# Seven products for a second set of K tiles in wout2, a new set in the second layer's glu1 and glu2, and down rows turned sooner

## The chip, the cores and the metric

One core of a Trainium2 chip runs the whole program in one launch. The metric is the device time of one execution in microseconds. An instruction runs on TensorE (PE, matrix products; PEld is its weight load), VectorE (DVE), ScalarE (ACT), GpSimd (POOL) or SyncE (SP); here POOL and SP mostly start DMAs. Each engine works through its own list in order and waits for others by semaphores. A matmul takes a stationary 128x128 block and a moving block of up to 512 columns and adds into a PSUM bank.

## The reference

Two layers, float32, 256 tokens, width 2048. With `h = rmsnorm(x)`:

```python
proj = h @ w_in          # conv a, glu, gate; q and kv down-projection (512 + 512 + 64); 3 more gates
y_conv = conv_branch(c_a, c_glu, c_gate, ...) @ w_proj_conv   # 31 taps over time, layernorm, silu, gate
y_mla = mla_branch(rmsnorm(q_down) @ w_uq, rmsnorm(kv_down) @ w_ukv, ...) @ w_proj_mla  # 16 heads
y = sigmoid(g_conv) * y_conv + sigmoid(g_mla) * y_mla
return x + y @ w_out     # the next layer's x
```

Nearly all the work is products of 256 token rows with weights that are each read once.

## The kernel before

**Blocks, ticks, units.** A layer is a list of blocks of 512 output columns (`order_of_layer`): glu0, down0 to down2 (512, 320 and 256 columns), glu1, glu2, the attention's uq and ukv with glu3 to glu7 between them, the gates, gmla, gconv, pmla, pconv and last wout0 to wout3. A block's weights come in eight pieces of two K tiles (`KS = 2`), 128x1024 float32, 512 KB, one DMA on SP each. A piece that is multiplied is a unit: ACT copies it into a rounded `hi`, DVE subtracts to get `lo`, and TensorE makes three products for each of the two token tiles and two K tiles, hi x hi, hi x (low half of the activations) and lo x hi: 12 matmuls of 128x512, one tick. `background` stands ahead of each tick. It runs what `at_slot` has put down for that tick (evacuations, transposes, stores and fetches, with tick distances written as numbers), and fills what is left of the tick with convolution work from a queue by estimated costs; `assist` lets ACT multiply taps of the convolution that DVE then only adds, while ACT's own estimate leaves more than a threshold. `InOrder` keeps this order on each engine, so an instruction that waits holds up all behind it on its engine.

**Seven products.** Two neighbouring blocks ("left" and "right"), two token tiles and two pieces make a 2x2 product of 2x2 block matrices. It is done with seven products instead of eight (42 matmuls, not 48). `q1, q7, q6, q5` begin the sums and need weights added to one another (DVE: `sum<-raw,raw`, `sum<-sum,raw`, `raw<-raw,raw`) and sums of the activations (`make_forms`: `whole`, `differences`, `forms`). They stand in the four ticks `TAIL` of the block ahead, the host. `q2, q4, q3` finish the four sums in ticks 0, 2, 4 (`front`) of the block itself; DVE joins the partial sums (`joins`, `right`). The banks alternate between two homes. `SEVEN` lists the left blocks: gconv0, gconv2, pconv2, wout0, wout2 in both layers. The pieces that are left are plain ticks, 12 for a pair of blocks. So wout0 (with wout1) hosts the beginning of wout2 (with wout3).

**Turning rows.** A result has tokens on partitions, and the next product needs columns there. `turn` stores a 128x512 tile to DRAM in four DMAs of 64 KB (`park`), fetches it back rearranged (`fetch`, 256 KB, POOL) `fetch_at` ticks later, and `at` ticks after the store DVE transposes it in 32x32 blocks (STREAM_TRANSPOSE). One tick behind that, halves are split off: for the next layer's input ACT writes `hT0` and DVE `hT1` (SCALAR_TENSOR_TENSOR, 128x128, four per token tile). The output blocks use it through `turn4` with c = 0 to 3 for the block and t for the token tile; block c's rows are K tiles 4c to 4c+3 of the next layer's glu0. The down rows are scaled by DVE (`scaled(0)` for q, `scaled(1)` for kv) and turned through `turn` in place; uq and ukv need them.

Of the kernel before, what the change touches and what calls it, by code (L numbers as in the profile page):

```python
# [19 lines left out]
P = 128  # L20
# [52 lines left out]
SEVEN = {(l, kind, i) for l in range(DEPTH) for kind, i in (("gconv", 0), ("gconv", 2), ("pconv", 2), ("wout", 0), ("wout", 2))}  # L73
# [47 lines left out]
def trunk(ctx: ExitStack, tc: tile.TileContext, xT, x, g_in, pos, win, wuq, wukv, wpc, wpm, wo, cst, rows, invf, out):  # L121
# [68 lines left out]
    TAIL = {n: (-7, -5, -4, -3) for n in (8, 12, 16)}  # L190

    def plan_all():
        blocks = [(l, k, i, pieces_of(l, s)) for l in range(DEPTH) for k, i, s in order_of_layer()]
        seven, home = None, 0
        for at, (l, k, i, block) in enumerate(blocks):
            first = (l, k, i) in SEVEN
            woven = WOVEN.get((l, k, i))
# [10 lines left out]
            block.twin = bool(first or woven)  # L208
            js = woven or js
            after = at + 1 + block.twin  # L210
            following = blocks[after] if after < len(blocks) else None
            tail = []
            if following and following[:3] in SEVEN:
                tail = ["q1", "q7", "q6", "q5"]
                upcoming = SimpleNamespace(units={}, home=1 - home, banks={}, forms=None)
                upcoming.n = following[3].n
                upcoming.left, upcoming.right = following[3].pieces[:2], blocks[after + 1][3].pieces[:2]
            tails = dict(zip([len(js) + a for a in TAIL[len(js)]], tail)) if tail else {}
            block.begins = upcoming if tail else None
            for slot, (j, right) in enumerate(js):  # L220
                tick = []
                for q, of in ((front.get(slot), seven), (tails.get(slot), upcoming if tail else None)):
                    if q:
                        (b11, b21), (b12, b22) = of.left, of.right
                        raw, unit = (lambda a: ("raw", a)), (lambda a: ("unit", of.units[a]))
                        if q in ("q1", "q2", "q3"):
                            if q == "q3":
                                sources.append(sources[b22])
                                b22 = len(sources) - 1
                            of.units[q] = plain({"q1": b11, "q2": b21, "q3": b22}[q])  # L230
                        elif q == "q7":
                            of.units[q] = summed(of.n, (raw(b12), raw(b22)), None, [b12, b22])
                        elif q == "q6":
                            of.units[q] = summed(of.n, (unit("q7"), raw(b11)), unit("q7"), [])
                        elif q == "q5":
                            of.units[q] = summed(of.n, (raw(b12), raw(b11)), raw(b12), [])
                        else:
                            of.units[q] = summed(of.n, (unit("q6"), raw(b21)), unit("q6"), [])
                        tick.append((q, of.units[q], of))
# [122 lines left out]
    def background(n, extra=0):  # L362
# [24 lines left out]
        while assist and budget["act"] > 0.8 and assist[0]():  # L387
            budget["act"] -= 0.85
# [86 lines left out]
    def one_of_seven(q, i, of):  # L475
# [3 lines left out]
        if q in ("q1", "q2", "q4"):  # L479
            parts = [of.stat({"q1": 0, "q2": KS, "q4": KS}[q] + kk, int(q == "q4")) for kk in range(KS)]  # L480
        else:
            parts = [of.forms(q, kk) for kk in range(KS)]
        hi, lo, _ = done[i]
        begins = q in ("q1", "q7", "q6", "q5")
        terms = [(kk, p) for p in range(3) for kk in range(KS)]
        for m, (kk, part) in enumerate(terms):
# [4 lines left out]
            )  # L491
        if q == "q1":
# [317 lines left out]
    for l in range(DEPTH):  # L810
# [31 lines left out]
        def down_after(down=down, qkc=qkc, ss_d=ss_d, r_d=r_d, kpe=kpe, ccq=ccq, ssq_t=ssq_t, gqk=gqk, row=row, C=C, ss_base=ss_base):  # L842
# [14 lines left out]
            def scaled(i):  # L857
                for t in range(T):
# [4 lines left out]
                    turn(d, LORA, None, then=lambda z, t=t: separated(i, t, z), then_costs=(0.65, 0.65), at=7 + t, home=d, fetch_at=3)  # L863
# [26 lines left out]
            at_slot(5, factors, 2.6)  # L890
# [840 lines left out]
```

## Time and profile before

| | us |
|---|---|
| median of 3 runs (lowest to highest) | 1865.14 (1865.07 to 1865.27) |
| profiled execution: time / span of its instructions | 1864.87 / 1863.1 |
| PE busy | 1857.7 (100%), 8395 matmuls |
| DVE busy | 1711.9 (92%), 2662 instructions |
| ACT busy | 1358.3 (73%) |
| POOL busy | 494.4 (27%) |
| granted TensorE clock | 1.0 |

Matmuls are pipelined: the durations of their rows overlap, so PE's pace is read from how many start in a stretch. DVE and ACT rows also overlap a little (a row's duration holds some 0.08 us that the next row shares). "Idle before <- releaser" in a timeline is the time an engine stood ahead of that row, and what let it go on. All rows of the program carry one line number (L132 before), since one helper issues every instruction, so rows are told apart by the tiles they write and read. An x8 behind a row stands for eight like rows in sequence.

### The profile page before, as it was taken

The numbers are of one execution on the slowest core, as the hardware profiler recorded it, in microseconds if no ns is written. First come the engines' busy times: TensorE is split into PE (matmuls) and PEld (weight loads), VectorE is DVE, ScalarE is ACT, GpSimd is POOL, SyncE is SP. The second block draws the span as 40 slices with busy tenths as digits, with TensorE's granted clock in tenths as the row PEclk, the third lists the DMA queues.
The fourth block names the chain that finished last, engine by engine and source line by source line (L and its number), as shares of the span: only waits on it lengthen the run. The fifth ranks groups of instructions, "written<-read, shape, count | busy, mean of one in ns | idle before, by whom it ended". The sixth has DMA issues, their size and how long they took to land.

```text
span 1863.1 us, 26923 instructions
## 1 busy us (share of the span) xinstructions
PE 1857.7 (100%) x8395; PEld 1544.7 (83%) x8395; DVE 1711.9 (92%) x2662; ACT 1358.3 (73%) x2421; POOL 494.4 (27%) x942
## 2 busy tenths in 40 slices
PE   9999999999999999999999999999999999999999
PEld 8888888888888888888888888888888888888887
DVE  6999999899999999999769999989999999988995
ACT  7678888988886765555657688888888777665553
POOL 0154555542200000021421545655322000000211
PEclk9999999999999999999999999999999999999999
DMA  8777877877755666678977777887877566765785
GB/s 333 234 267 246 275 253 253 266 268 232 238 200 199 206 220 218 204 244 277 333 233 232 258 263 260 257 257 257 273 237 235 189 198 209 235 216 184 252 279 178
DMA packets 140400, 450.28 MB, mean 242 GB/s; under 512 B 23840, under 2 KB 29216, under 8 KB 140256
## 3 DMA queue, kind: packets, MB, share of 16 engines
q1 hardware_dynamic: 106416, 364.74, 59.2%
q0 software_dynamic: 32832, 82.62, 13.5%
q8 instruction: 66, 1.08, 0.2%
q10 hardware_dynamic: 1008, 1.20, 0.2%
q14 instruction: 78, 0.64, 0.1%
HBM read 404.43 MB, written 44.04 MB: 241 GB/s over the span
## 4 chain that ended last, share of the span: by engine, by line
PE 98%; DVE 2%; issue 0%; DVEq 0%
PE acc L132 73%; PE left L132 12%; PE right L132 11%; PE o_ps L132 1%; PE s1w L132 1%; DVE lo L132 1%; PE s L132 1%; DVE v_t L132 1%; PE warm L132 0%; PE acc_end L132 0%; DVE whole_a L132 0%; DVE sum L132 0%; DVE whole_b L132 0%; DVE form_b L132 0%; DVE forms L132 0%
## 5 line engine op out<-in xcount | busy, mean ns | idle before, releaser
L132 ACT CAST hi<-raw 128x1024 fp32r<-128x1024 f32 (+2 forms) x683 | 695.3, 1028 | 302.0 <-PE acc L132 168.0
L132 DVE TENSOR_TENSOR lo<-raw,hi 128x1024 fp32r<-128x1024 f32 (+2 forms) x667 | 798.9, 1204 | 95.4 <-ACT hi L132 32.3
L132 PE MATMUL acc<-hi,hT 128*128 128x512 f32 (+1 forms) x1472 | 357.7, 383 | 0.0
L132 PEld LDWEIGHTS acc<-hi,hT 128*128 128x128 f32 x1472 | 271.5, 188 | 53.5
L132 PE MATMUL acc<-hi,h_hi 128*128 128x512 f32 (+1 forms) x736 | 224.8, 386 | 0.0
L132 PE MATMUL acc<-hi,h_lo 128*128 128x512 f32 (+2 forms) x736 | 220.6, 381 | 0.0
L132 DVE SCALAR_TENSOR_TENSOR v_t<-u_t,cst,v_t 128x256 f32<-128x256 f32 x500 | 213.8, 479 | 2.9
L132 ACT ACTIVATE tap<-u_t,cst 128x256 f32<-128x256 f32 x460 | 200.7, 499 | 7.4 <-DVE v_t L132 7.4
L132 POOL DMA_DIRECT2D turned<-turn_d x88 | 49.2, 559 | 558.8 <-DVE v_t L132 362.2
L132 PE MATMUL acc<-lo,h_hi 128*128 128x512 f32 (+1 forms) x704 | 189.9, 386 | 0.0
L132 PE MATMUL acc<-lo,hT 128*128 128x512 f32 (+1 forms) x704 | 189.3, 386 | 0.3 <-DVE lo L132 0.3
L132 POOL DMA_DIRECT2D turn_d<-gate x184 | 100.2, 551 | 285.6 <-DVE gate L132 177.1
L132 DVE TENSOR_TENSOR v_t<-v_t,tap 128x512 f32<-128x512 f32 x230 | 157.8, 686 | 6.5
L132 PEld LDWEIGHTS acc<-hi,h_lo 128*128 128x128 f32 x736 | 137.4, 188 | 28.1 <-DVE h_lo L132 0.2
L132 PEld LDWEIGHTS acc<-hi,h_hi 128*128 128x128 f32 x736 | 135.9, 188 | 26.1 <-ACT h_hi L132 0.3
L132 PEld LDWEIGHTS acc<-lo,hT 128*128 128x128 f32 x704 | 131.1, 188 | 26.9 <-DVE lo L132 0.7
L132 PEld LDWEIGHTS acc<-lo,h_hi 128*128 128x128 f32 x704 | 130.9, 188 | 26.7 <-DVE lo L132 0.8
L132 PE MATMUL acc<-hi,oT 128*128 128x512 f32 x512 | 127.8, 389 | 0.0
L132 PE MATMUL acc<-hi,qkc 128*128 128x512 f32 x448 | 115.4, 389 | 0.0
L132 PEld LDWEIGHTS acc<-hi,oT 128*128 128x128 f32 x512 | 95.8, 188 | 19.7
L132 PEld LDWEIGHTS acc<-hi,qkc 128*128 128x128 f32 x448 | 83.5, 188 | 17.0
L132 POOL DMA_DIRECT2D turn_d<-su x128 | 70.0, 553 | 104.3 <-DVE su L132 89.1
(259 smaller groups left out, 2877.2 us busy)
## 6 DMA issues: line engine op xcount, KB each, us to landing
raw<-in_win SPq DMA_DIRECT2D x401, 512.0 KB, 4.3
raw<-in_wo SPq DMA_DIRECT2D x68, 512.0 KB, 5.5
raw<-in_wpc SPq DMA_DIRECT2D x66, 512.0 KB, 4.3
raw<-in_wpm SPq DMA_DIRECT2D x64, 512.0 KB, 3.6
raw<-in_wukv SPq DMA_DIRECT2D x32, 512.0 KB, 4.4
turned<-turn_d POOLq DMA_DIRECT2D x56, 256.0 KB, 4.7
raw<-in_wuq SPq DMA_DIRECT2D x24, 512.0 KB, 4.3
turn_d<-qk POOLq DMA_DIRECT2D x128, 96.0 KB, 4.5
```

Source lines behind the costliest of these rows:

```text
L132: ins = getattr(self.engine, name)(*a, **k)
```

## The change

Two groups of seven in wout2 (16 of 32 piece products of its pair, in place of 8) in both layers, with the two groups' sums joined only once; one group in the second layer's glu1 and glu2, begun in down0 of that layer and held in its banks over down1 and down2; the second group's forms in tiles of the pool `uv`; residual rows of c >= 2 in that pool too; c=1 of the output blocks turned at 5 ticks instead of 8; the second layer's down rows scaled one tick sooner, fetched 2 instead of 3 ticks after the store and turned 4 instead of 7; the assist threshold 0.4 instead of 0.8.

```diff
-SEVEN = {(l, kind, i) for l in range(DEPTH) for kind, i in (("gconv", 0), ("gconv", 2), ("pconv", 2), ("wout", 0), ("wout", 2))}
+SEVEN = {(l, kind, i): n for l in range(DEPTH) for kind, i, n in (("gconv", 0, 1), ("gconv", 2, 1), ("pconv", 2, 1), ("wout", 0, 1), ("wout", 2, 2))}
+SEVEN[1, "glu", 1] = 1
+BEGUN_IN = {("glu", 1): ("down", 0)}
...
-    TAIL = {n: (-7, -5, -4, -3) for n in (8, 12, 16)}
+    COMMON, OTHERS = ("q1", "q7", "q6", "q5"), ("q2", "q4", "q3")
+    TAIL = {1: ((-7, -5, -4, -3),), 2: ((-10, -9, -8, -7), (-6, -5, -4, -3))}
+    FRONT = {1: ((0, 2, 4),), 2: ((0, 2, 4), (1, 3, 5))}
...
-                js = js[2:] + [(j, True) for j, _ in js[2:]]
+                js = js[2 * quads :] + [(j, True) for j, _ in js[2 * quads :]]
...
-        while assist and budget["act"] > 0.8 and assist[0]():
+        while assist and budget["act"] > 0.4 and assist[0]():
...
+        begins = q in COMMON and quad is of.quads[0]
...
+        if quad is not of.quads[-1]:
+            return
         if q == "q1":
...
+                parts = [uv_p.tile([P, KS, SEQ], F32R, tag="uv", name=f"form{p}") for p in range(4)]
...
+            soon = int((l, "glu", 1) in SEVEN)
...
-                    turn(d, LORA, None, then=lambda z, t=t: separated(i, t, z), then_costs=(0.65, 0.65), at=7 + t, home=d, fetch_at=3)
+                    turn(d, LORA, None, then=lambda z, t=t: separated(i, t, z), then_costs=(0.65, 0.65), at=(4 if soon else 7) + t, home=d, fetch_at=3 - soon)
...
-            at_slot(5, factors, 2.6)
+            at_slot(5 - soon, factors, 2.6)
             for i in range(2):
-                at_slot(6 + 2 * i, lambda i=i: scaled(i), 1.3)
+                at_slot(6 - soon + (2 - soon) * i, lambda i=i: scaled(i), 1.3)
...
-                soon_at = {} if c == 1 else dict(fetch_at=3, at=6)
-                return turn(src, 512, None, then=use, then_costs=costs, **soon_at)
+                return turn(src, 512, None, then=use, then_costs=costs, fetch_at=at[c] // 2, at=at[c])
...
+                pool, tag = (uv_p, "uv") if c >= 2 else (wide_p, "w")
+                keep["x", c, t] = pool.tile([P, 512], F32, tag=tag, name="xres")
...
-            turn4(xt, c, t, use, 1.15, 1.3)
+            turn4(xt, c, t, use, 1.15, 1.3, at=(6, 5, 6))
...
-                product(pl, uses_h, lambda t, ps, i=i: glu_evac(i, t, ps), at, (0.9, 2.2), tardy=6 if i == 0 and l else None)
+                product(pl, uses_h, evac_of(glu_evac, i, pl), at, (0.9, 2.2), tardy=6 if i == 0 and l else None)
...
-                    at_slot(8, lambda i=i, f=wout_begin: f(i + 1))
+                    at_slot(len(pl.ticks) - 4, lambda i=i, f=wout_begin: f(i + 1))
```

Over the program TensorE gets 18 matmuls of 128x512 fewer (8377 for 8395), VectorE 15 instructions more (2677 for 2662), and SP three loads of 512 KB more.

Three places show how the order moves. DVE in the first layer's wout0, before (a row names what is written and what is read; the number behind a unit's `lo` counts units, and `raw` numbers are pieces):

```order
L132 TENSOR_TENSOR lo325_8708<-raw318_8604,hi325_8682 128x1024
L132 TENSOR_TENSOR gate_8726<-right_8088,sc_6647 128x512
L132 TENSOR_TENSOR gate_8726<-gate_8726,ym_5812 128x512
L132 STREAM_TRANSPOSE turned_8642<-turned_8642 128x512
L132 TENSOR_TENSOR yT1_8139<-turned_8619,yT0_8138 128x4x128
L132 TENSOR_TENSOR lo326_8737<-raw319_8628,hi326_8710 128x1024
L132 TENSOR_TENSOR lo327_8749<-raw683_8652,hi327_8739 128x1024
L132 TENSOR_TENSOR yT1_8139<-turned_8642,yT0_8138 128x4x128
L132 TENSOR_TENSOR lo328_8773<-raw312_8672,hi328_8751 128x1024
```

and the same place of the changed kernel:

```order
L134 TENSOR_TENSOR lo325_8744<-raw324_8638,hi325_8718 128x1024
L134 TENSOR_TENSOR sum327_8748<-raw332_8686,raw333_8688 128x1024
L134 TENSOR_TENSOR gate_8762<-right_8122,sc_6687 128x512
L134 TENSOR_TENSOR gate_8762<-gate_8762,ym_5838 128x512
L134 STREAM_TRANSPOSE turned_8676<-turned_8676 128x512
L134 TENSOR_TENSOR yT1_8173<-turned_8653,yT0_8172 128x4x128
L134 TENSOR_TENSOR lo326_8773<-raw318_8662,hi326_8746 128x1024
L134 TENSOR_TENSOR lo327_8785<-sum327_8748,hi327_8775 128x1024
L134 TENSOR_TENSOR lo328_8798<-raw319_8708,hi328_8787 128x1024
L134 TENSOR_TENSOR sum327_8748<-sum327_8748,raw324_8638 128x1024
L134 TENSOR_TENSOR whole_a_8817<-yT0_8172,yT1_8173 128x512
L134 TENSOR_TENSOR whole_b_8819<-yT0_8172,yT1_8173 128x512
```

The first common product (unit 325) now stands in the stage's first ticks, and its sums of weights and the second group's `whole` rows come between the low halves. Before, the first sum of weights came three rows below the last row shown.

DVE in the second layer's glu0, before (turned_9328 and 9330 are the rows of output block c=2, turned_9453 and 9455 of c=3; hT1 is the low half of the layer's input, which TensorE reads):

```order
L132 SCALAR_TENSOR_TENSOR hT1_8999<-turned_9328,gains_111,hT0_8998 128x128 x4
L132 SCALAR_TENSOR_TENSOR hT1_8999<-turned_9330,gains_111,hT0_8998 128x128 x4
L132 TENSOR_TENSOR lo359_9473<-raw344_9313,hi359_9437 128x1024
L132 TENSOR_TENSOR lo360_9491<-raw345_9344,hi360_9475 128x1024
L132 STREAM_TRANSPOSE turned_9453<-turned_9453 128x512
L132 STREAM_TRANSPOSE turned_9455<-turned_9455 128x512
L132 TENSOR_TENSOR lo361_9511<-raw346_9370,hi361_9493 128x1024
```

and in the changed kernel (c=2 in turned_9448 and 9450, c=3 in turned_9513 and 9515):

```order
L134 STREAM_TRANSPOSE turned_9448<-turned_9448 128x512
L134 STREAM_TRANSPOSE turned_9450<-turned_9450 128x512
L134 TENSOR_TENSOR lo363_9537<-raw345_9385,hi363_9519 128x1024
L134 STREAM_TRANSPOSE turned_9513<-turned_9513 128x512
L134 STREAM_TRANSPOSE turned_9515<-turned_9515 128x512
L134 SCALAR_TENSOR_TENSOR hT1_9098<-turned_9448,gains_111,hT0_9097 128x128 x4
L134 SCALAR_TENSOR_TENSOR hT1_9098<-turned_9450,gains_111,hT0_9097 128x128 x4
L134 TENSOR_TENSOR lo364_9573<-raw346_9420,hi364_9539 128x1024
```

The rows of c=2 that write hT1 stood four rows ahead of c=3's first transpose and now stand behind its second. On POOL the two fetches of c=2 move in the same way; before:

```order
L132 DMA turned_9328<-turn_d_9244 128x512
L132 DMA turn_d_9386<-xres_9286 32x4x128 x4
L132 DMA x1_dram_106<-xres_9286 128x512
L132 DMA x1_dram_106<-xres_9288 128x512
L132 DMA turned_9453<-turn_d_9386 128x512
```

and in the changed kernel:

```order
L134 DMA turn_d_9436<-xres_9286 32x4x128 x4
L134 DMA turned_9448<-turn_d_9324 128x512
L134 DMA turned_9450<-turn_d_9331 128x512
L134 DMA x1_dram_106<-xres_9286 128x512
L134 DMA x1_dram_106<-xres_9288 128x512
L134 DMA turned_9513<-turn_d_9436 128x512
```

The fetch of c=2 stood ahead of the store of c=3's rows and now stands behind it.

DVE where the second layer's down rows are turned, before (down1 holds the rows; two transposes for q, then two for kv; qkc1 is their low half):

```order
L132 TENSOR_TENSOR lo401_10444<-raw386_10302,hi401_10426 128x1024
L132 STREAM_TRANSPOSE down1_9403<-down1_9403 128x512
L132 TENSOR_TENSOR lo402_10467<-raw387_10334,hi402_10446 128x1024
L132 STREAM_TRANSPOSE down1_9403<-down1_9403 128x512
L132 TENSOR_TENSOR qkc1_9404<-down1_9403,qkc1_9404 128x4x128
L132 TENSOR_TENSOR lo403_10488<-raw388_10377,hi403_10469 128x1024
L132 STREAM_TRANSPOSE down1_9403<-down1_9403 128x512
```

and in the changed kernel:

```order
L134 TENSOR_TENSOR lo407_10522<-raw386_10387,hi407_10499 128x1024
L134 TENSOR_TENSOR kpe_9469<-ka_10237,kb_10238 128x2x32
L134 TENSOR_TENSOR kpe_9469<-kb_10238,ka_10237 128x2x32
L134 SCALAR_TENSOR_TENSOR ccq_9470<-cos2_109,down1_9465 128x128
L134 SCALAR_TENSOR_TENSOR ssq_t_9471<-sin2_110,down1_9465 128x128
L134 SCALAR_TENSOR_TENSOR gqk_9472<-cst_9464 128x1
L134 STREAM_TRANSPOSE down1_9465<-down1_9465 128x512
L134 TENSOR_TENSOR lo408_10549<-raw387_10399,hi408_10524 128x1024
L134 STREAM_TRANSPOSE down1_9465<-down1_9465 128x512 x2
L134 TENSOR_TENSOR qkc1_9466<-down1_9465,qkc1_9466 128x4x128
L134 TENSOR_TENSOR lo409_10571<-raw388_10429,hi409_10551 128x1024
```

The first transpose now comes four ticks behind the scaling of q, where it came seven behind, and the first of kv shares a tick with the second of q.

More of the change, by code (lines that the diff above doesn't have):

```diff
@@ L206, in plan_all @@
                 if k == "wout" and i == 0:
                     js.sort(key=lambda e: e[0] // 2)
[L208 to L239, printed above, removed]
@@ new lines, in plan_all @@
+            block.plain, block.twin, block.seven, block.begins = woven or js, bool(quads or woven), None, None
+            block.extra = [[] for _ in block.plain]
+            block.begun_in = block
+        home = 0
+        for at, (l, k, i, block) in enumerate(blocks):
+            if skipped(at) or (l, k, i) not in SEVEN:
+                continue
+            host = at - 1
+            while skipped(host) or (k, i) in BEGUN_IN and blocks[host][1:3] != BEGUN_IN[k, i]:
+                host -= 1
+            host = blocks[host][3]
+            home = 1 - (host.seven.home if host.seven else 0)
+            of = block.seven = host.begins = SimpleNamespace(kind=k, home=home, banks={}, first=None, last=None)
+            number = SEVEN[l, k, i]
+            of.quads = [
+                SimpleNamespace(
+                    of=of, c=c, n=block.n, units={}, left=block.pieces[2 * c : 2 * c + 2],
+                    right=blocks[at + 1][3].pieces[2 * c : 2 * c + 2],
+                )
+                for c in range(number)
+            ]
+            for quad, tail, front in zip(of.quads, TAIL[number], FRONT[number]):
+                for q, a in zip(COMMON, tail):
+                    host.extra[len(host.plain) + a].append((q, quad))
+                for q, a in zip(OTHERS, front):
+                    block.extra[a].insert(0, (q, quad))
@@ L240, in plan_all @@
+        for at, (l, k, i, block) in enumerate(blocks):
+            if skipped(at):
+                continue
+            for (j, right), extra in zip(block.plain, block.extra):
+                tick = [unit_of_seven(q, quad) for q, quad in extra]
                 tick.append((right, plain((blocks[at + 1][3] if right else block).pieces[j]), j))
                 block.ticks.append(tick)
-            if tail:
-                seven = upcoming
         return blocks
@@ L479, in one_of_seven @@
         if q in ("q1", "q2", "q4"):
-            parts = [of.stat({"q1": 0, "q2": KS, "q4": KS}[q] + kk, int(q == "q4")) for kk in range(KS)]
+            parts = [of.stat(2 * KS * quad.c + (KS if q != "q1" else 0) + kk, int(q == "q4")) for kk in range(KS)]
         else:
-            parts = [of.forms(q, kk) for kk in range(KS)]
+            parts = [quad.forms(q, kk) for kk in range(KS)]
         hi, lo, _ = done[i]
-        begins = q in ("q1", "q7", "q6", "q5")
+        begins = q in COMMON and quad is of.quads[0]
         terms = [(kk, p) for p in range(3) for kk in range(KS)]
@@ L840, in down_evac, with down_after @@
                 act.activation(dst, ps, AF.Copy, scale=r)
[L842 removed]
+        def down_after(l=l, down=down, qkc=qkc, ss_d=ss_d, r_d=r_d, kpe=kpe, ccq=ccq, ssq_t=ssq_t, gqk=gqk, row=row, C=C, ss_base=ss_base):
             ka = work.tile([P, T, ROPE], F32, tag="qa", name="ka")
@@ L1531, in trunk, with forms_of, forms_at @@
         h_parts = h_hi, h_lo
-        ready = {"gmla": lambda: h_parts, "gconv": lambda: h_parts, "pconv": lambda: keep["yc"], "wout": lambda: keep["y"]}
+        ready = {"pconv": lambda: keep["yc"], "wout": lambda: keep["y"]}
         forms = {}
+        def forms_of(of, quad, begin):
+            family = "h" if of.kind in ("gmla", "gconv") else of.kind
+            parts = ready.get(of.kind, lambda: h_parts)
+            if (family, quad.c) not in forms:
+                forms[family, quad.c] = make_forms(parts, begin, quad.c)
+            quad.forms = forms[family, quad.c]
+        def forms_at(of, quad, ticks):
+            return ticks + TAIL[len(of.quads)][quad.c][1] - (5 if ticks == 8 else 4)
         for at_block, (kind, i, pl) in enumerate(planned):
```

69 lines of the change are left out of this document (39 added, 30 removed).

## The prediction

> **What bounds the kernel now.** I read the page's busy shares and chain first, then the waits of TensorE, then windows by stage, then the timelines of the engines that deliver to TensorE.
>
> ```profile
> PE 1857.7 (100%) x8395; PEld 1544.7 (83%) x8395; DVE 1711.9 (92%) x2662; ACT 1358.3 (73%) x2421; POOL 494.4 (27%) x942
> ...
> PE 98%; DVE 2%; issue 0%; DVEq 0%
> ...
> PE right L132 <- DVE lo L132: 0.5, 1, 0.5
> PE acc L132 <- DVE lo L132: 0.3, 1, 0.3
> ```
>
> TensorE (PE) is busy for all of the span, the chain runs through it for 98%, and it waited for VectorE (DVE) only 0.8 us in all. So fewer matmuls shorten the run, if every other engine still delivers in time. DVE at 92% is an average. By stage (windows: PE, PEld, DVE, ACT, POOL busy, clock, DMA share, GB/s):
>
> ```profile
> 813.00:855.00 42.00, 42.00 (x186) 34.64 (x185) 41.66 (x51) 22.95 (x28) 11.00 (x20) 1.00 0.77 256
> 855.00:897.00 42.00, 42.00 (x186) 34.61 (x185) 37.95 (x42) 23.45 (x30) 7.03 (x13) 1.00 0.83 279
> 932.40:954.00 21.60, 21.60 (x97) 17.88 (x96) 16.65 (x30) 14.15 (x29) 4.57 (x9) 1.00 0.75 251
> 954.00:976.00 22.00, 22.00 (x99) 18.22 (x98) 12.19 (x24) 9.76 (x12) 5.50 (x10) 1.00 0.71 232
> 1739.00:1781.00 42.00, 42.00 (x186) 34.62 (x185) 41.66 (x51) 22.93 (x27) 10.97 (x20) 1.00 0.78 253
> 1781.00:1824.00 43.00, 43.00 (x191) 35.43 (x190) 38.84 (x45) 24.05 (x27) 5.49 (x10) 1.00 0.81 282
> ```
>
> The last projection begins at about 812 us in the first layer and 1739 us in the second, the output projection at 855 and 1781, the second layer's gate block at 932.4, its first down block at 954. In both 813:855 and 1739:1781 DVE works 41.66 of 42.00 us: it enters the output projection with no reserve of time, only with the few low halves (`lo`) that it is ahead by. PE's 42.00 us hold 186 matmul rows of 128x512; two are under way at a time, so the pace is 42.00/185 = 0.227 us.
>
> **The gain.** Each added group of seven products drops 6 matmuls of 48: three groups (one in each layer's wout2, one in the second layer's glu1), 18 x 0.227 = -4.1 us. All else can only cost, since PE had 0.8 us of waits to give back.
>
> **wout0, both layers: DVE falls behind.** The host of wout2's common products has 12 ticks as before but now 8 common units in them: two more sums of 128x1024 with their `lo`, plus a second set of forms.
>
> ```profile
> 825.09 0.42 DVE L132 TENSOR_TENSOR whole_b<-whole_a,whole_b 128x256 f32<-128x256 f32 x1
> ...
> 826.80 2.36 DVE L132 TENSOR_TENSOR lo<-raw,hi 128x1024 fp32r<-128x1024 f32 x2
> ...
> 856.70 0.68 DVE L132 TENSOR_TENSOR gate<-right,sc 128x512 f32<-128x512 f32 x1
> 857.42 0.69 DVE L132 TENSOR_TENSOR gate<-gate,ym 128x512 f32<-128x512 f32 x1
> 858.02 0.70 DVE L132 STREAM_TRANSPOSE turned<-turned 128x512 f32<-128x512 f32 x1
> 858.65 0.67 DVE L132 TENSOR_TENSOR right<-right,joins 128x512 f32<-128x512 f32 x1
> 859.23 1.20 DVE L132 TENSOR_TENSOR lo<-raw,hi 128x1024 fp32r<-128x1024 f32 x1
> 860.36 0.68 DVE L132 TENSOR_TENSOR gate<-right,sc 128x512 f32<-128x512 f32 x1
> ...
> 871.43 1.23 DVE L132 TENSOR_TENSOR sum<-raw,raw 128x1024 f32<-128x1024 f32 x1 [1.67 <-DMA raw<-in_wo]
> ...
> 863.26 1.07 PE L132 MATMUL right<-lo,yT 128*128 128x512 f32 x4
> ```
>
> From start to start: `lo` and sums of 128x1024 1.13 us (859.23 to 860.36), 128x512 adds 0.60 (857.42 to 858.02), a gate product 0.72, a transpose 0.63, the four half-width rows of the `whole` group 1.71 (825.09 to 826.80). Low half 325 of before is the row at 859.23; it ends at 860.43 and PE uses it at 863.26, so DVE is ahead by 2.83. In the order of the change the same place is a common product, whose `lo` is used 4 matmuls sooner: 2.83 - 0.91 = 1.9 us ahead. From there to `lo339` DVE has 20 rows of 128x1024 (22.6), two gate rows (1.3), three transposes (1.9), eight adds (4.8) and the four small ones (1.7): 32.3 us. PE has 120 matmuls, 27.2 us. 1.9 - (32.3 - 27.2) = -3.2: PE stalls 3.2 us in all before DVE catches up in the last four ticks, whose units are plain. Whole stage by the same durations: DVE 39.7 before, 51.5 after, PE 42.2 and 47.6. The second layer enters with the same fill (41.66 again), so 2 x 3.3 = +6.6, with 0.1 each for a restart. Bounds: DVE waited 1.67 us here at 871.43 for a weight that SP had sent late. If those loads come no later in program order but meet the extra loads, each layer pays up to 1.2 more (9 together); if DVE is a tick further ahead than this row, 0.9 less (5 together). wout2 itself loses DVE work (31.4 to 31.2 against PE 30.0) and starts ahead by more than the excess: nothing.
>
> **Layer boundary, glu0: rows of c=2 wait behind c=3.** wout2 has 8 ticks, not 12, so the fetches of output block c=2's transposed rows come, on POOL, behind c=3's stores, and on DVE the eight `hT` rows of c=2 come behind c=3's two transposes.
>
> ```profile
> 934.96 1.30 DVE L132 STREAM_TRANSPOSE turned<-turned 128x512 f32<-128x512 f32 x2
> ...
> 937.28 2.19 DVE L132 SCALAR_TENSOR_TENSOR hT<-turned,gains,hT 128x128 fp32r<-128x128 f32 x8
> ...
> 946.01 0.71 DVE L132 STREAM_TRANSPOSE turned<-turned 128x512 f32<-128x512 f32 x1 [3.94 <-DMA turned<-turn_d]
> 947.27 0.71 DVE L132 STREAM_TRANSPOSE turned<-turned 128x512 f32<-128x512 f32 x1 [0.55 <-DMA turned<-turn_d]
> ...
> 929.87 0.55 POOL L132 DMA_DIRECT2D turned<-turn_d  x1 [1.63 <-DVE hT L132]
> 933.61 2.20 POOL L132 DMA_DIRECT2D turn_d<-xres  x4 [3.19 <-DVE xres L132]
> 935.79 1.12 POOL L132 DMA_DIRECT2D x_dram<-xres  x2
> 939.36 1.17 POOL L132 DMA_DIRECT2D turned<-turn_d  x2 [2.44 <-DMA turn_d<-xres]
> ...
> 943.30 1.98 PE L132 MATMUL acc<-hi,hT 128*128 128x512 f32 x8
> ```
>
> Before, c=2 was fetched at 927.68 and 929.87, transposed at 934.96 and split at 937.28, long before PE's fifth tick at 943.30. c=3 left POOL at 933.61, was fetched at 939.36 and kept DVE waiting 3.94 and 0.55 us, to 947.98; nobody suffered, since c=3 is used two ticks later. Now DVE's order puts c=2's split behind that second transpose: earliest 947.98 + 0.35 for its first row + 0.1. PE needs `hT1` of c=2 from the third pair of matmuls of the tick at 943.30, at 943.75. Stall 948.4 - 943.75 = 4.6. Two fetches of 256 KB more now share those microseconds, so I take 5.0. Lower bound: only the first of the two waits matters (946.01, and a fetch 2 us quicker): 1.3. Upper: fetches lengthened by half the medians below: 7.5.
>
> ```profile
> turned<-turn_d POOLq DMA_DIRECT2D x56, 256.0 KB, 4.7
> down<-turn_d POOLq DMA_DIRECT2D x8, 256.0 KB, 5.4
> ```
>
> A rule that speaks for less is in the Trainium skill, "DMA: Bandwidth & Descriptors", section "Anatomy of one DMA — SWDGE (gpsimd) path": a DMA costs about 2.0 us and its bytes by 436 GB/s, which would be 2.6 us for 256 KB, an estimate from that page. By it the stall would be about 2 us smaller; the rows above say 4.7 and 5.4 us under this load, and the rows are used.
>
> **glu1: the down rows are turned 4 ticks after scaling.** Chain on POOL: 16 parks (64 KB stores), q's two fetches, 8 parks of `su`, kv's two fetches. Its order is unchanged; what moved is DVE, which meets the transposes sooner.
>
> ```profile
> 1017.23 1.41 DVE L132 SCALAR_TENSOR_TENSOR down<-down,r_d 128x512 f32<-128x512 f32 x2
> ...
> 1034.30 1.22 DVE L132 TENSOR_TENSOR lo<-raw,hi 128x1024 fp32r<-128x1024 f32 x1
> ...
> 1040.95 0.71 DVE L132 STREAM_TRANSPOSE down<-down 128x512 f32<-128x512 f32 x1 [0.25 <-DMA down<-turn_d]
> ...
> 1018.26 4.35 POOL L132 DMA_DIRECT2D turn_d<-down  x8 [51.13 <-DVE down L132]
> ...
> 1028.67 1.12 POOL L132 DMA_DIRECT2D down<-turn_d  x2 [0.32 <-issue]
> ...
> 1035.78 0.55 POOL L132 DMA_DIRECT2D turn_d<-su  x1 [0.90 <-DMA down<-turn_d]
> 1036.32 1.12 POOL L132 DMA_DIRECT2D down<-turn_d  x2
> ...
> 1041.08 1.07 PE L132 MATMUL acc<-lo,hT 128*128 128x512 f32 x4
> ```
>
> Count from S, the first scaling (1017.23): first park S+1.0, q fetched at S+11.4 and, at 5.4 each, landed by S+17; the last `su` parks wait for that landing (1035.78), so kv is fetched at S+19.1 and its first transpose starts at S+23.7 (1040.95, 0.25 of it waiting). In the new order DVE reaches kv's first transpose after 13.4 us of rows from S. Behind it stand a 0.63 transpose (ending S+24.4), a 0.60 add and `lo409` (1.13): S+26.1. `lo` runs 4.8 to 5.6 us ahead there (1034.30 + 1.22 against 1041.08 gives 5.6; three buffers allow no more): `lo404`, done at S+2.5, is used at S+7.3, and `lo409` five ticks of 12 matmuls (13.6) later, S+20.9. Stall 5.2; kv's second row, 0.7 later, adds about 0.7 with `lo410`. The second scaling now follows at once rather than 4.4 us later, which can bring the parks forward by about 0.5: 5.5 taken. Lower bound 1.9: parks leave at POOL's pace of 0.54 (4.35/8) without the pauses and fetches land 1.5 us quicker. Upper 7.5: queued behind the second group's weights.
>
> **Edits with one answer.** The glu1 group's common products fall in the first down block, where DVE works 12.19 of 22.00 us; 11 us more fits. Lower assist threshold: 68 multiply-adds of 0.479 leave DVE, 34 adds of 0.686 come (-9 us) and ScalarE takes the taps at 73% fill. Where PE waited before in the gconv groups (most of the 0.8 us) I take +0.3, bounds -0.4 and +1.0. Turning c=1 of the output projection 5 ticks behind its sum, not 8, and residual rows in another pool of buffers move transfers that nobody in those stages waits for in the trace: nothing. Three more loads of 512 KB run in stages at 0.71 to 0.83 DMA share: nothing of their own.
>
> **Sum**, against the profiled execution's own 1864.87 us (span 1863.1): -4.1 + 6.6 + 5.0 + 5.5 + 0.3 = +13.3, so 1878.2. That execution lies 0.27 below the median 1865.14.
>
> **Rivals.**
> All absorbed: faster. DVE's extra work in wout0 would have to fit in what it is ahead by and the fetches land within their ticks; then 1864.87 - 4.1 = 1860.8. It decides at DVE 5.1 us ahead on entry to wout0, instead of the 1.9 worked out; for it speaks that PE hardly waits today, against it 41.66 of 42.00. Chance 0.08.
> Only wout0: POOL's chains land in time because the earlier stalls give them time. 1864.87 - 4.1 + 6.6 = 1867.4. Against: the chains start from PE's own results and stalls upstream move both. 0.10.
> One of the two fetch stalls only: 1872.4 to 1872.9. 0.10.
> More than forecast: each long stall also slows the matmuls behind it. The start of the trace has such a phase:
>
> ```profile
> 0.78 4.18 PE L132 MATMUL warm<-const-float32-0.0 128*128 128x256 f32 x19 [0.78 <-PEq L1720]
> ```
>
> 19 matmuls of 256 columns take 4.18 us, 0.22 each, as long as 512 columns take later. If that returned behind each of the two 5 us stalls for 3.4 to 4.2 us, at half pace, each costs 1.7 to 2.1 more: 1882. Nothing in before shows it, as PE never stood for 1 us. 0.15.
> The Trainium skill, "TensorE: Matmul & The Clock Gate", Part 1, states it as a rule: an idle window of about 3.4 us puts the clock to half until a busy one has passed; no run here shows such a stall yet.
>
> **Chances.** The forecast as it stands 0.57, own range 1873 to 1882. About 0.2%, 3.7 us, is what a measurement of this kernel can tell from no change: the only-wout0 case (+0.13%) counts as the same, 0.10; faster 0.08; slower 0.82. The range from 1867 to 1885 takes in only-wout0 at the foot and, at the top, the slow-clock case with the upper bounds of one term.
>
> **What would show it.** Right: PE waits named `lo` in wout0 (855 to 905, about 1790 to 1842), about 3 us in each; a wait of about 5 us for `hT` some 11 us into the second layer's glu0, with DVE idle there for `turned`; a wait of 5 to 6 us in glu1, with DVE idle for `down<-turn_d`. PE busy rows 18 fewer. Wrong: DVE idle in wout0; c=2's transposes landing before c=3's stores leave; kv's fetch issued less than 14 us after the first scaling; granted clock below 1.00 behind the stalls.

## The result and the profile after

| | before | changed |
|---|---|---|
| median, us (lowest to highest) | 1865.11 (1864.65 to 1865.27) | 1885.82 (1884.67 to 1886.58) |
| ratio, 95% interval | | 1.0111 (1.0093 to 1.0128) |
| profiled execution / span | 1864.87 / 1863.1 | 1885.13 / 1883.4 |
| granted TensorE clock | 1.0 | 0.996 |

The change is slower by 20.7 us, where +13.3 was forecast; the time lies 0.8 us outside the range. The page of the changed kernel:

```profile
PE 1863.0 (99%) x8377; PEld 1543.1 (82%) x8377; DVE 1743.0 (93%) x2677; ACT 1393.6 (74%) x2506; POOL 494.1 (26%) x942
...
PE 95%; DVE 2%; DMA 1%; issue 1%; POOL 0%; ACT 0%; DVEq 0%; POOLq 0%
```

There are 18 matmuls fewer, as counted, and yet PE is busy 5.3 us longer: some of its matmuls ran slower. TensorE's waits (in total, times, longest):

```profile
PE acc L134 <- DVE hT L134: 6.7, 1, 6.7
PE left L134 <- DVE lo L134: 4.5, 6, 1.2
PE acc L134 <- DVE qkc L134: 2.9, 2, 1.8
PE right L134 <- DVE lo L134: 1.9, 6, 0.5
```

It waited 16.0 us in place of 0.8. All three places that the prediction named are there: `lo` (6.4, of which 1.2 in the gconv groups and 0.2 in glu1), `hT` (6.7), and the down rows (2.9, named `qkc` and not `lo`).

Where the time went is best read by following the same matmul through both traces. One matmul early in each stage starts at 857.37 before and 857.59 after in the first layer's wout0 (0.2 late), 935.14 and 938.04 in glu0 (2.9), 956.90 and 968.62 in down0 (11.7), 1052.87 and 1070.21 in the first ukv block (17.3), 1784.08 and 1801.89 in the second layer's wout0 (17.8); the whole is 20.3 late. The saved matmuls (1.36 per group) must be added back, so the stages cost 0.2 (up to wout0), 4.0 (first wout0), 8.8 (layer boundary), 7.0 (down0 to uq0), 0.5 (the second layer's gconv) and 3.8 (second wout0 and the end), less 4.1 for 18 matmuls: 20.2.

**wout0.** The window of the first layer's stage (PE, PEld, DVE, ACT, POOL busy, clock, DMA share, GB/s) and the four longest of its five stalls on PE (the fifth, at 871.84, is 0.25 us by the start times):

```profile
855.00:912.00 57.00, 54.46 (x235) 43.31 (x234) 54.48 (x62) 31.39 (x40) 10.83 (x20) 1.00 0.76 254
```

```profile
865.49 1.20 PE L134 MATMUL right<-lo,yT 128*128 128x512 f32 x4 [0.49 <-DVE lo L134]
...
876.97 1.21 PE L134 MATMUL left<-lo,yT 128*128 128x512 f32 x4 [1.16 <-DVE lo L134]
...
891.57 0.73 PE L134 MATMUL right<-lo,form 128*128 128x512 f32 x2 [0.19 <-DVE lo L134]
...
893.84 1.21 PE L134 MATMUL left<-lo,yT 128*128 128x512 f32 x4 [0.62 <-DVE lo L134]
```

The first row for which DVE itself waits is

```profile
889.69 0.69 DVE L134 TENSOR_TENSOR yT<-turned,yT 128x512 fp32r<-128x512 f32 x1 [0.58 <-ACT yT L134]
```

DVE works 54.48 of 57.00 us and up to 889.69 waits for nothing: it sets the pace here. A stall costs more than its wait: by the start times the matmul next behind each came 0.34 us later and not 0.227.

**Layer boundary.** First DVE, then POOL, then PE of the changed kernel:

```profile
945.12 0.71 DVE L134 STREAM_TRANSPOSE turned<-turned 128x512 f32<-128x512 f32 x1 [2.88 <-DMA turned<-turn_d]
947.16 0.71 DVE L134 STREAM_TRANSPOSE turned<-turned 128x512 f32<-128x512 f32 x1 [1.33 <-DMA turned<-turn_d]
...
951.47 0.71 DVE L134 STREAM_TRANSPOSE turned<-turned 128x512 f32<-128x512 f32 x1 [2.49 <-DMA turned<-turn_d]
952.78 0.71 DVE L134 STREAM_TRANSPOSE turned<-turned 128x512 f32<-128x512 f32 x1 [0.60 <-DMA turned<-turn_d]
953.41 2.15 DVE L134 SCALAR_TENSOR_TENSOR hT<-turned,gains,hT 128x128 fp32r<-128x128 f32 x8
```

```profile
936.95 2.20 POOL L134 DMA_DIRECT2D turn_d<-xres  x4 [4.27 <-DVE xres L134]
939.14 1.13 POOL L134 DMA_DIRECT2D turned<-turn_d  x2
...
942.08 1.16 POOL L134 DMA_DIRECT2D turned<-turn_d  x2 [0.74 <-DMA turn_d<-xres]
```

```profile
953.78 2.93 PE L134 MATMUL acc<-hi,hT 128*128 128x512 f32 x6 [6.67 <-DVE hT L134]
```

and the DMA view of c=3's two fetches (count, size, median us from issue to landing), before and then changed:

```profile
turned<-turn_d POOLq DMA_DIRECT2D x2, 256.0 KB, 6.9
...
turned<-turn_d POOLq DMA_DIRECT2D x2, 256.0 KB, 9.7
```

c=3's stores (936.95) stand ahead of c=2's fetches (939.14), as the order said, and the eight rows of c=2 (953.41) stand behind c=3's second transpose (952.78). c=3 was fetched at 942.08 and transposed at 951.47 and 952.78: 9.7 us of flight, where before it was 6.9. PE stood 6.67 us. Of the two orders that changed, the one on DVE cost more: c=2's own second transpose began at 947.16, so without c=3's transposes ahead of it the split could have begun some 4.5 to 5.5 us sooner, an estimate from these rows. Then the clock, in windows of 1 us (PE busy and its matmuls, clock, DMA share, GB/s):

```profile
950.00:951.00 1.00, 0.00 (x0) 0.66 1.03 410
...
957.00:958.00 1.00, 1.00 (x6) 0.93 0.41 78
```

The mean of 0.66 puts the fall to 0.50 at about 950.3, 3.2 us after PE's last matmul ended (947.1), and the mean of 0.93 puts the rise at 957.1, 3.4 us after PE had gone on. In that stretch matmuls start every 0.427 us, not 0.227: 8 late matmuls, 1.7 us by the start times. The Trainium skill, "TensorE: Matmul & The Clock Gate", Part 1, gives half the clock after an idle window of about 3.4 us and full clock after a busy one; this fall and this rise fit it, at 3.2 and 3.4 us, and the next fall does not.

**Down rows.** First q's low half on DVE before, then DVE, POOL and PE of the changed kernel:

```profile
1038.58 0.65 DVE L132 TENSOR_TENSOR qkc<-down,qkc 128x512 fp32r<-128x512 f32 x1
```

```profile
1035.99 1.41 DVE L134 SCALAR_TENSOR_TENSOR down<-down,r_d 128x512 f32<-128x512 f32 x2
...
1052.42 0.71 DVE L134 STREAM_TRANSPOSE down<-down 128x512 f32<-128x512 f32 x1 [5.49 <-DMA turn_d<-su]
...
1056.88 0.71 DVE L134 STREAM_TRANSPOSE down<-down 128x512 f32<-128x512 f32 x1 [2.02 <-DMA down<-turn_d]
1057.52 0.65 DVE L134 TENSOR_TENSOR qkc<-down,qkc 128x512 fp32r<-128x512 f32 x1
```

```profile
1037.03 4.36 POOL L134 DMA_DIRECT2D turn_d<-down  x8 [56.13 <-DVE down L134]
...
1047.36 1.12 POOL L134 DMA_DIRECT2D down<-turn_d  x2
...
1053.72 1.12 POOL L134 DMA_DIRECT2D down<-turn_d  x2
```

```profile
1058.22 1.21 PE L134 MATMUL acc<-hi,qkc 128*128 128x512 f32 x4 [1.81 <-DVE qkc L134]
1060.55 1.22 PE L134 MATMUL acc<-hi,qkc 128*128 128x512 f32 x2 [1.12 <-DVE qkc L134]
```

S, the start of the first scaling, is 1035.99. The first store came at S+1.0 and q's fetch at S+11.4, as forecast, and q's first row was transposed at S+16.4, where its landing was put at S+17; kv was fetched at S+17.7 and transposed at S+20.9, where S+19.1 and S+23.7 were forecast. The `lo` row behind q's first transpose came 0.2 us late. PE waited for another row: q's low half (`qkc`, 1057.52) stands behind kv's transpose, where before it stood ahead of it (1038.58, and kv's transpose at 1040.95), and uq0's third matmul needs it. The `lo` behind it (1058.09), uq0's own, was then not waited for. PE had two waits, 1.81 and 1.12, and a slow clock behind them:

```profile
1059.00:1060.00 1.00, 0.43 (x2) 0.77 0.00 0
1060.00:1061.00 1.00, 0.45 (x1) 0.50 0.63 119
...
1066.00:1067.00 1.00, 1.00 (x5) 0.81 0.89 309
```

It was halved from 1059.5 to 1066.4: 14 late matmuls, 2.8 us by the start times. Four matmuls ran between the two waits, and the clock fell all the same: PE need not stand still for the whole time.

### The profile page after: what moved, and what is told of

Read it like the earlier page. It is cut to its first block, busy times and chain, and to the rows that moved or that the text cites. A ratio compares the mean times of both kernels' runs of the same rounds, so it can differ in the third digit from the quotient of the medians.

```text
span 1883.4 us, 26986 instructions
## 1 busy us (share of the span) xinstructions
PE 1863.0 (99%) x8377; PEld 1543.1 (82%) x8377; DVE 1743.0 (93%) x2677; ACT 1393.6 (74%) x2506; POOL 494.1 (26%) x942
## 4 chain that ended last, share of the span: by engine, by line
PE 95%; DVE 2%; DMA 1%; issue 1%; POOL 0%; ACT 0%; DVEq 0%; POOLq 0%
PE acc L134 71%; PE left L134 12%; PE right L134 10%; DVE lo L134 1%; PE o_ps L134 1%; PE s1w L134 1%; PE s L134 1%; DMA turned<-turn_d 1%; POOL turn_d L134 0%; DVE v_t L134 0%; DVE raw L134 0%; PE warm L134 0%; DMA down<-turn_d 0%; DVE whole_a L134 0%; DMA turn_d<-xres 0%
## 5 line engine op out<-in xcount | busy, mean ns | idle before, releaser
L134 PE MATMUL acc<-hi,hT 128*128 128x512 f32 (+2 forms) x1344 | 327.6, 384 | 6.7 <-DVE hT L134 6.7
L134 PEld LDWEIGHTS acc<-hi,hT 128*128 128x128 f32 x1344 | 248.3, 188 | 56.1 <-DVE hT L134 7.0
L134 ACT ACTIVATE tap<-u_t,cst 128x256 f32<-128x256 f32 x528 | 229.9, 501 | 10.2 <-DVE v_t L134 10.0
L134 DVE TENSOR_TENSOR v_t<-v_t,tap 128x512 f32<-128x512 f32 x264 | 181.2, 686 | 7.9
L134 DVE SCALAR_TENSOR_TENSOR v_t<-u_t,cst,v_t 128x256 f32<-128x256 f32 x432 | 184.5, 479 | 2.4
L134 PE MATMUL acc<-lo,hT 128*128 128x512 f32 (+1 forms) x640 | 172.1, 386 | 0.0
L134 PEld LDWEIGHTS acc<-lo,hT 128*128 128x128 f32 x640 | 119.5, 188 | 24.0
```

The costliest lines, as they stand in the source:

```text
L134: ins = getattr(self.engine, name)(*a, **k)
```

## Experiments

A table first; below it each run. The middle columns are worked out from each run's own trace: the start-to-start times of the matmuls less 0.227 us each, summed from 855 to 915 us (first wout0), 915 to 970 (boundary and the beginning of down0) and 1030 to 1075 (glu1 to uq0). "Of filling" is what the added matmuls take at 0.227 us each. Each ratio below is to runs of the kernel before that were taken beside the run.

| kernel | median us | wout0 | boundary | glu1 to uq0 |
|---|---|---|---|---|
| before | 1865.11 | 0.2 | 0.0 | 0.0 |
| changed | 1885.82 | 4.2 | 8.8 | 6.8 |
| c=2 one tick sooner | 1880.20 | 4.1 | 3.6 | 5.2 |
| waits filled with matmuls | 1883.04 | 4.1 | 7.7 with 5.9 of filling | 3.4 with 1.6 |
| c=2 one tick sooner, kv stored by SP | 1880.46 | 4.2 | 3.8 | 6.8 |
| second group without sums | 1884.01 | 2.7 | 9.3 | 7.0 |
| second group without forms | 1880.54 | 1.1 | 10.0 | 5.4 |
| one group in wout2 | 1873.44 | 0.2 | 2.7 | 8.4 |
| no group in glu1 | 1880.43 | 4.2 | 9.7 | 0.0 |
| assist 0.8 | 1885.84 | 4.1 | 8.7 | 8.0 |
| sums on GpSimd | 1891.75 | 6.9 | 10.4 | 5.2 |
| one group in wout2, down rows turned later | 1872.09 | 0.2 | 2.8 | 2.3 |
| one group in wout2, all turns reordered | 1870.15 | 0.2 | 2.9 | 1.9 |
| the last, assist and c=1 as before | 1869.58 | 0.2 | 3.3 | 2.4 |

**Is it c=2 behind c=3?**

```diff
-            turn4(xt, c, t, use, 1.15, 1.3, at=(6, 5, 6))
+            turn4(xt, c, t, use, 1.15, 1.3, at=(6, 5, 5))
```

> The changed kernel with output block c=2 turned one tick sooner (at 5, fetch at 2), so that on POOL its fetches stand ahead of c=3's stores again and on VectorE its split rows stand ahead of c=3's transposes. Theory (the wait of 6.7 us for hT comes from that order): wait and the half-clock phase behind it go, 8.8 us less, 1877. Rival (four fetches and two stores at once are what is slow, so c=2 still lands late): at least 3 us of the wait stay, 1880 or more.

The median is 1880.20, its ratio to before 1.0080 (1.0065 to 1.0095). The wait for `hT` is gone, and the clock is full there: the theory holds. The gain was 3 us less than hoped, for another wait that had been covered. DVE and PE's waits in this kernel:

```profile
942.50 2.18 DVE L134 SCALAR_TENSOR_TENSOR hT<-turned,gains,hT 128x128 fp32r<-128x128 f32 x8
...
949.17 0.71 DVE L134 STREAM_TRANSPOSE turned<-turned 128x512 f32<-128x512 f32 x1 [3.35 <-DMA turned<-turn_d]
950.63 0.71 DVE L134 STREAM_TRANSPOSE turned<-turned 128x512 f32<-128x512 f32 x1 [0.75 <-DMA turned<-turn_d]
```

```profile
PE acc L134 <- DVE lo L134: 2.3, 2, 1.2
```

c=2 is split at 942.50. DVE then waits 3.35 and 0.75 us for c=3, as it did before the change, but now goes straight into the extra rows of the glu1 group in down0 (forms, sums) and PE gets two low halves late, 1.3 and 1.5 us with the restarts. c=3's flight, with c=2's fetches out of its way, was 7.0 and 7.5 us. In the last column, some 1.1 us of the gain is the clock alone: behind two waits, as in the changed kernel, it stayed halved for 3.4 us (1055.0 to 1058.4) and not 6.8.

**Is the clock lost by standing still?**

```diff
+                if fill_in and j == fill_in[0] and (t, kk, part) == (0, 0, 1):
+                    ...
+                    for m in range(fill_in[2]):
+                        pe.matmul(spare[:, :n], sh, hi[:, 0, :], start=True, stop=True)
```

> The changed kernel with 26 matmuls whose result nobody reads put into the wait for hT in glu0 and 7 into the first wait for qkc in uq0. Theory (TensorE's clock falls because it stands still): clock 1.00 throughout, 1.7 us less behind the first wait and 2.8 less behind the second, 1881.3; the waits themselves end when they ended. Rival (the matmuls behind the waits are slow for another reason, such as their operands): no time saved, 1885 to 1887, clock as before.

The median is 1883.04 (1.0098, 1.0083 to 1.0113), 2.8 less than the changed kernel with 33 matmuls more. PE at the first place, and windows over both (PE busy and matmuls, clock, DMA share, GB/s):

```profile
947.71 6.10 PE L134 MATMUL fill<-hi,hT 128*128 128x512 f32 x26
954.43 1.81 PE L134 MATMUL acc<-hi,hT 128*128 128x512 f32 x6 [0.63 <-DVE hT L134]
```

```profile
947.00:958.00 11.00, 10.29 (x43) 1.00 0.69 274
1056.00:1067.00 11.00, 9.81 (x42) 1.00 0.65 215
```

The clock is 1.00 in both, and the six matmuls behind the wait take 1.81 us where they took 2.93: idleness is the cause, and the rival falls. In the two places 4.5 us were saved, as forecast in sum, though not place by place (8.8 to 7.7 and 6.8 to 3.4, where 1.7 and 2.8 less were expected); some 2 came back later, in the attention behind, where PE waited 1.2 us for `su`, a row of the convolution's input on DVE, which no longer had the slow stretch to catch up in. That last reason is argued only.

**Does VectorE's time make the stalls in wout0?** Two kernels leave out part of the second group's work. The first multiplies unsummed weights, the second takes the first group's sums of activations:

```diff
+        if not u.skip:
+            vec.tensor_add(dst, *(value(key) for key in u.terms))
```

> The changed kernel without the four additions of weights of the second group in each layer (it multiplies unsummed weights instead): VectorE has three rows of 1.14 us less in each wout0, one less in each wout2; matmuls and loads are the same. Theory (VectorE is short of time in wout0): stalls of 4.0 us in each wout0 fall by 3.0 to 3.4, 1879 to 1880. Rival (the low halves are late because weights land late): within 1 us of 1885.8.

```diff
+            c = 0
-            if (family, quad.c) not in forms:
+            if (family, c) not in forms:
```

> The changed kernel in which the second group of wout2 uses the first group's sums of activations, so VectorE makes no second set: eight rows less per layer (two of 0.60 and four small ones of 1.71 together early in wout0, two of 0.60 later), ScalarE two less; matmuls, loads and weight sums are the same. Theory (VectorE is short of time in wout0, early as well as late): the first three of the five stalls in each wout0 (2.7 us with their restarts) go, and the last two shrink, so 3 to 4 us less per layer, 1878 to 1880. Rival (the early stalls come from late weights or from the first group's sums): the early stalls stay, 1884 or more.

Without sums it is 1884.01 (1.0101, 1.0086 to 1.0116): each wout0 costs 1.45 less, half of what was expected. The last two of the five stalls went, and the first three, which stand ahead of these sums, stayed to a hundredth. Without forms it is 1880.54 (1.0081, 1.0067 to 1.0094): 4.2 fell to 1.1 in each, and one stall of five was left, the first and not, as expected, the last two shrunk; the total is 0.5 above what was expected, with 1.2 more at the boundary. PE's waits for `lo` over the whole run, of which only one of 0.5 per layer is in wout0 (866.55 and 1807.93) and the others are in the gconv groups:

```profile
PE right L134 <- DVE lo L134: 1.3, 3, 0.5
PE left L134 <- DVE lo L134: 1.0, 2, 0.6
```

So four of the five stalls go with the VectorE rows that stand ahead of them, with the same loads and matmuls; late weights are out for these. The first stall, 0.8 of the 4.2 us with its restart, stays in both kernels and goes only with one group in wout2, below. That it too is VectorE's time is argued from the DVE rows ahead of it, which stand without a wait.

**Which part of the change costs what?**

```diff
-("wout", 2, 2))}
+("wout", 2, 1))}
```

> The changed kernel with one group of seven in wout2 instead of two, in both layers (wout2 has 12 ticks again). Theory (wout0 short of VectorE, and c=2 behind c=3 because wout2 is short): the 4.2 us of stalls in each wout0 and the 8.8 at the layer boundary go, 12 matmuls (2.7) come back, and the 2.9 us of late low halves in down0 that showed when c=2 was turned sooner come in: 1885.8 - 8.4 - 8.8 + 2.7 + 2.9 = 1874. Rival (the boundary's wait comes from the group in glu1 and its loads): hT still waits by 3 us or more, 1878 or more.

```diff
-SEVEN[1, "glu", 1] = 1
```

> The changed kernel without the group in the second layer's glu1, and the down rows turned at 7 as before. Theory (glu1 with four ticks fewer leaves the down rows' chain uncovered): 6.8 us of waits and slow clock at uq0 go, 6 matmuls (1.4) come back: 1880.4; the wait for hT stays at 6 to 7 us. Rival (the slow clock at uq0 is a late effect of the first long wait): 2 to 3 us of slow clock stay there, 1883.

```diff
-        while assist and budget["act"] > 0.4 and assist[0]():
+        while assist and budget["act"] > 0.8 and assist[0]():
```

> The changed kernel with the assist threshold back at 0.8. Theory (fewer multiplications on VectorE but more taps on ScalarE, small stalls in the gconv groups 1.4 us more than before): 1 to 1.5 us less, 1884.5. Rival (the gconv stalls come from something else, or VectorE's lighter load helps elsewhere): within 0.5 us of 1885.8 or above.

One group in wout2: 1873.44 (1.0045, 1.0028 to 1.0062), as worked out: both wout0 run clean, the wait for `hT` is gone, and down0's late halves appear. No group in glu1: 1880.43 (1.0083, 1.0068 to 1.0098), as worked out; the clock at uq0 is full although the long wait at the boundary is still there, so the second slow stretch is of its own place. Assist: 1885.84, no difference; the excess around the gconv groups did shrink (by the start times 1.05 to 0.91 us from 500 to 855 and 1.31 to 0.67 from 1500 to 1780), but the wait at uq0 was 1.2 longer in this profile.

**Can the down rows be had in time?** First, with c=2 sooner, kv's stores go to another queue; then, with one group in wout2, the turns come later:

```diff
-... home=d, fetch_at=3 - soon)
+... home=d, fetch_at=3 - soon, queue=sp if soon and i else gps)
```

> As the kernel with c=2 turned sooner, and kv's down rows stored by SP instead of POOL, so POOL fetches q after 8 stores instead of 16. Theory (the chain of 16 stores, two fetches, 8 stores, two fetches on POOL sets the end of glu1): q lands some 4 to 5 us sooner, the 6.9 us of waits and slow clock there go, 1870. Rival (SP's stores hold up the weights behind them, about 3.6 us): a wait for weights takes their place, 1874 or more.

The median is 1880.46 (1.0084, 1.0067 to 1.0100), no better than with c=2 sooner alone. DVE and POOL:

```profile
1042.33 0.70 DVE L134 STREAM_TRANSPOSE down<-down 128x512 f32<-128x512 f32 x1
...
1053.16 0.71 DVE L134 STREAM_TRANSPOSE down<-down 128x512 f32<-128x512 f32 x1 [6.56 <-DMA down<-turn_d]
1053.79 0.65 DVE L134 TENSOR_TENSOR qkc<-down,qkc 128x512 fp32r<-128x512 f32 x1
```

```profile
1046.06 0.55 POOL L134 DMA_DIRECT2D turn_d<-su  x1 [2.52 <-DMA down<-turn_d]
1047.03 1.25 POOL L134 DMA_DIRECT2D down<-turn_d  x2 [0.42 <-DMA raw<-in_wukv]
```

q's first row no longer waits, at S+10.9 (S is 1031.47). But kv's fetch comes behind stores of `su`, one of which waits 2.52 us for a buffer that q's fetch must free first; it leaves at 1047.03, lands 6.1 us later, and q's split (1053.79) stands behind kv's transpose as before. This is neither the theory nor the rival: the queue was relieved, the order on DVE was not.

```diff
-... at=(4 if soon else 7) + t, home=d, fetch_at=3 - soon)
+... at=((5, 6)[i] if soon else 7) + t, home=d, fetch_at=3 - soon)
```

> As the kernel with one group in wout2, with q's down rows turned 5 ticks and kv's 6 ticks behind the scaling (4 and 4 there). Theory (q's low half stands on VectorE behind kv's transposes, which wait for the last fetch): q's split no longer waits for kv's fetch, the wait for qkc (4.9) falls below 1.5 and the clock stays 1.00, 6 to 8 us less: 1866 to 1867.5. Rival (q's own fetch is late): the wait for qkc stays above 3, 1871 or more.

```profile
PE acc L134 <- DVE lo L134: 2.2, 2, 1.2
PE acc L134 <- ACT qkc L134: 1.1, 1, 1.1
...
PE acc L134 <- DVE qkc L134: 0.4, 1, 0.4
```

With one group in wout2 the profiled execution is 5.4 us shorter (1875.95 to 1870.52), the wait for DVE's `qkc` fell from 4.9 to 0.4 and the clock stayed full: the order was the cause of that wait. The median, 1872.09 (1.0036, 1.0023 to 1.0049), is only 1.4 below the kernel with one group. The clock differs between executions of one kernel: with one group the profiled one was the slowest of four, with a mean clock of 0.998 and the others 0.999 to 1.000, and here two (1869.65 and 1870.52) had 1.000 and three (1872.09 to 1873.29) 0.999. So the waits that are left still cost a slow clock in some executions, and how much of the gain is lasting stays open.

**Is there a version that gains?**

```diff
-... at=(4 if soon else 7) + t, home=d, fetch_at=3 - soon)
+... at=((5, 6)[i] if soon else 7) + t, home=d, fetch_at=3 - 2 * soon, queue=sp if soon and i else gps)
-... - (5 if ticks == 8 else 4)
+... - (5 if ticks == 8 and of.kind != 'glu' else 4)
```

> As the kernel with one group in wout2, with q's rows turned at 5 and kv's at 6, both fetched one tick behind the store, kv's stores on SP, and the glu1 group's sums of activations one tick later. Theory (order alone makes the waits): no wait above 1 us in glu0, down0, glu1 and uq0, so before's time less 6 matmuls plus 1.5 in the gconv groups: 1865. Rival (the group in down0 leaves VectorE short behind c=3's transposes whatever the order): 2 to 3 us of late low halves stay there, 1868.

> As the last, with the assist threshold at 0.8 and c=1 of the output blocks turned at 8 as before, so that only the glu1 group and its turns differ from the kernel before. Theory: 1864.9 - 1.4 = 1863.5, plus what of the late low halves in down0 stays. Rival: those stay by 2 to 3 us, 1866.

The medians are 1870.15 (1.0026, 1.0016 to 1.0037) and 1869.58 (1.0024, 1.0014 to 1.0033), both still slower than before. In the second:

```profile
PE acc L134 <- DVE qkc L134: 1.4, 2, 1.1
PE left L134 <- DVE forms L134: 1.3, 1, 1.3
PE acc L134 <- DVE lo L134: 1.0, 1, 1.0
```

Both came out by the rival, and above it: the group in down0 and glu1 saves 1.4 us of matmuls and costs 3.3 in stalls at the boundary and 2.4 at uq0. The kernel before stays the fastest.

```diff
-        vec.tensor_add(dst, *(value(key) for key in u.terms))
+        (gps if u.skip else vec).tensor_add(dst, *(value(key) for key in u.terms))
```

> The changed kernel with the second group's four weight additions in each layer made by GpSimd instead of VectorE. Theory (only VectorE's time matters): as the kernel without these additions, 1884.0, if GpSimd takes up to 3 us for one. Rival (GpSimd is slower than the ticks allow, or slows VectorE beside it): the waits for these units grow, 1887 or more.

The median is 1891.75 (1.0145, 1.0130 to 1.0160), by the rival. GpSimd's group (busy, mean ns; idle before):

```profile
L134 POOL TENSOR_TENSOR raw<-raw,raw 128x1024 f32<-128x1024 f32 x8 | 21.4, 2687 | 33.6 <-DMA raw<-in_wo 26.0 <-issue 7.6
```

GpSimd takes 2.69 us for a sum that VectorE makes in 1.22. In the first wout0 it made the last two from 888.73 to 894.32, where VectorE had made them from 886.75 to 892.65, and wout0 went from 4.2 to 6.9. What held the first of the two until 888.73 is not shown: the profile gives its 7.62 us of idle time to no wait.

## Why the prediction was right and wrong

The direction and the three places were right; the time is some 7 us above the sum. The step that failed is a cost: the sum put the slow matmuls behind the two long stalls at nothing and left them to a rival, and they took 4.5 us. Next come c=3's fetch, 2.8 us longer in the air where 0.4 was allowed, and the restarts of the stalls. In glu1 the prediction had the wrong row waiting.

- **Gain, 18 matmuls, -4.1.** Right.
- **wout0, +6.6: 8.0 by the start times (4.2 less before's 0.2, twice).** The shortage of VectorE was sized well: in each layer the five gaps at the stalls hold 3.36 us above 0.227 each, against 3.2 worked out from rows of before. Under-sized was what a stall costs beyond itself: one restart of 0.1 per layer was counted, and there are five, a second late matmul behind each stall.
- **Boundary, +5.0: measured 8.8.** The place, the order and the tick were right. Two terms were too small. c=3's fetch was given 0.4 us more for its new neighbours and took 2.8 more (9.7 against 6.9). And the slow clock behind the wait, 1.7 us over 8 matmuls, was put among the rivals.
- **glu1, +5.5: measured 7.0.** The chain on POOL came within 0.1 us up to q's fetch. What failed here is the step that named the victim: the fetch of kv was quicker by 1.4 us in the air and 1.4 in its issue, and not `lo409` but the row ahead of it, q's `qkc` behind kv's transpose, was waited for; the sum counted it as a row of DVE but not as one that uq0 needs first. The stalls came to 4.0 us where 5.5 was taken, and the slow clock added 2.8 (14 matmuls). So the term was nearer than its parts, by luck.
- **"11 us more fits" in down0.** Wrong as argued, by the mean of a stage: DVE has the room, but behind its own wait for c=3. In the changed kernel the long stall covered it; it showed at 2.7 us with one group in wout2 and at 3.5 with c=2 sooner, once that was gone.
- **Assist and gconv, +0.3.** It was 0.5 in the second layer and 0.2 in all up to the first wout0, within its bounds.
- **Chances.** Slower was given 0.82. The rival with a slow clock, 1882 with 0.15, is the one that happened, and a clock below 1.00 behind the stalls was among the prediction's own signs of being wrong; its two stretches cost 4.5 together against 3.4 to 4.2 given to it, and the longer flight and the restarts took the time beyond 1885.

## What to carry to other kernels

Where an engine has no reserve of time, a change that saves on TensorE and adds to that engine must be summed row by row from the last place where its lead is known, with a restart for every stall and not for the sum. When a stage is shortened, list every instruction that stands on a clock of ticks behind it, on every queue: the two large losses here are not the added work but rows that changed places behind a DMA. A stall of some 3 us or more has to be priced with the slow matmuls behind it, and so may two shorter ones close together.

## What was not expected of the hardware

The clock fell to 0.50 behind two waits of 1.81 and 1.12 us with four matmuls between them; a single wait of 1.16 us, as in wout0, left it at 1.00. In both falls of the changed kernel it stayed halved for 6.8 us, and matmuls of 512 columns started every 0.427 us. That is twice the window of about 3.4 us which the Trainium skill, "TensorE: Matmul & The Clock Gate", Part 1, names.

The kept traces record each change of the clock. Within a trace all changes lie whole multiples of 3.413 us apart, and the clock stayed halved for 3.4 us (c=2 one tick sooner), 6.8 us (the changed kernel) or 10.2 us (at the boundary of the kernel without the second group's forms). Cut each trace, from its first change on and without its last 5 us, into stretches of 3.413 us on its own grid, and count 0.227 us for each matmul. Ahead of each of the 14 falls PE then worked at most 1.26 us of the stretch, and in every other stretch at full clock at least 1.37 us. Counted with 0.427 us a matmul, it worked at least 3.2 us of the stretch ahead of each rise, and at most 2.5 where the clock stayed halved. So whether shorter stalls cost clock depends on where they fall on the grid: in wout0 of the kernel with sums on GpSimd, waits of 0.99 and 1.74 us with four matmuls between them left it at 1.00. Why the grid is so is not shown.

c=3's fetch of 256 KB, beside three others and two stores of that size, took 9.7 us, where its kind has a median of 4.9 in the changed kernel.
